# The last two experts' outputs combined on chip, the next layer's first weights and the sums loaded under the last products, a second buffer for the last activations

## The chip, the cores and the metric

One core of a Trainium2 chip runs the whole program in one launch. The metric is the device time of one execution in microseconds (us). The kernel before takes 1949.7 us, the median of three runs (1946.35 to 1953.62).

## The reference, cut to what matters

Two layers of a backbone, each a token mixer (three groups of heads) and an expert-choice channel mixer, run for 512 latent and 128 context tokens of width 1024. The change lies in the channel mixer and in the layer norm behind it:

```python
def _expert_choice(h, w_router, w_gate_up, w_down):
    aff = jax.nn.softmax((h @ w_router).astype(F32), axis=-1)
    gate, idx = lax.top_k(jnp.swapaxes(aff, 1, 2), cap)      # 16 experts; 64 latent, 16 context tokens each
    def per_request(hb, ib, gb):
        xe = hb[ib]
        a, b = jnp.split(jnp.einsum('ecd,edf->ecf', xe, w_gate_up), 2, axis=-1)
        ye = jnp.einsum('ecf,efd->ecd', jax.nn.silu(a) * b, w_down) * gb[..., None].astype(hb.dtype)
        return jnp.zeros_like(hb).at[ib.reshape(-1)].add(ye.reshape(-1, hb.shape[-1]))
...
x = _layernorm(alpha * x + g2 * ff, ln2_g[l], ln2_b[l])      # then the next layer's projection of x
```

## The kernel before, in words

All weights are float32 and come from HBM in tiles of 128x2048 (1 MB), into a pool of 25 slots (`Slots`); `Halves` hands out halves of a slot. `Ahead` holds the list of tiles to come; `fill(n, keep)` issues loads on SP's queue as long as fewer than n are held and more than `keep` slots are free. A slot is free again when its last matmul is done.

**The experts** (`moe`). For each of 16 experts e (e0 to e15): POOL gathers its 80 token rows by an indirect DMA (`gather`), VectorE turns them (`turned_x`, in 32x32 blocks, `squares`), `gate_up` multiplies them with eight tiles of gate and up weights (`wgu`) into PSUM, and ScalarE and VectorE make the activations `act`. One expert later, `turned_act` turns them into `aTs`, the only buffer for turned activations, and `down` multiplies with four tiles `wdn` into two PSUM banks `pl` (latent) and `pc` (context). `lat` (L1681) are the latent matmuls, `cxt` (L1685) the context ones. `down` ends on VectorE: gate and modulation for the latent half (L1739), for the context half (L1743, L1746), all into `y`. POOL adds `y` to the running sums `acc` in HBM by an indirect DMA with addition (L1754). `down(e-1)` is issued behind `gate_up(e)`.

**The last expert** before the change is not scattered. Its `y` is split into a high and a low part (`split`, L344 on ScalarE and L345 on VectorE) and added on chip: `combine(t)` makes each of the five token tiles t in PSUM as identity times `acc` (L1834, L1832) plus a one-hot matrix times `yh` (L1835) and `yl` (L1836). The one-hot rows come from comparing an `iota` table with the chosen indices (`places`, `one_hot`). The five tiles of `acc` are read back from HBM by SP's queue (L1814), behind the scatter of e14.

**The layer norm and the next layer's start** (`ln2`). Per tile: `ln_stats` (two bn_stats L608, bn_aggr L610, a reciprocal root on POOL L392, `nmr` L614), the normalisation on ScalarE (L1882), then behind layer 0 the turn by TensorE (L626), modulation (L631, L633) and a split (`hT_tile`: `hhi`, `hlo`, `hcx`; L344, L345), the store of x with its gains on POOL (L1902, L1905), and the first projection `tile_A` (L348 to L350) with the first weight tile of layer 1 (`first_w`: `win` split into `wh` and `wl` in four pieces). Behind layer 1 gains and offsets (L1884, L1885 on POOL and VectorE) and the stores to the outputs follow. `OR1` and `OR2` order these steps over the tiles.

What sets the order on an engine is the scheduler of the language, from the data and from `issue_after(x)`, which holds an instruction back until x has been issued. Each engine then works strictly in that order, and SP's queue too.

## Time and profile before

| what | value |
|---|---|
| median of three runs | 1949.7 us |
| the profiled execution's own time | 1953.35 us |
| its span, from first to last instruction | 1951.6 us |
| TensorE busy | 1807.9 us (93%) |
| VectorE, ScalarE, POOL busy | 1151.8, 417.7, 224.5 us |
| moved by DMA | 555 MB, 284 GB/s over the span |
| granted TensorE clock, mean | 0.957 of full |

The profiled execution is 3.65 us above the median, and 1.75 us of it lie around the span. A busy share is a mean over stages with different limits: in the experts' stage TensorE and the DMA engines are both full, and at the two ends of layers neither is.

### The profile page before, as it was taken

What the parts mean: (1) busy time and instruction counts of PE and PEld (TensorE: products, weight loads), DVE (VectorE), ACT (ScalarE), POOL (GpSimd) and SP (SyncE); (2) the same over time, 40 slices, a digit from 0 to 9 for tenths busy, and PEclk for the clock granted to TensorE, in tenths of its full rate; (3) what the DMA queues carried; (4) which work ended last, traced back from release to release, by engine and by line L of the source; (5) the groups of instructions that cost most, each with busy time, mean ns of one, the idle gap of its engine ahead of it and who ended that gap; (6) DMA issues with size and microseconds to landing.
All of it is one profiled execution on the core that took longest, in us unless ns stands there. A gap on an engine that the chain in (4) does not pass through costs nothing. (4 is left out here: it accounts for less than half of the span.)

```text
span 1951.6 us, 34372 instructions
## 1 busy us (share of the span) xinstructions
PE 1807.9 (93%) x14135; PEld 903.2 (46%) x14135; DVE 1151.8 (59%) x2966; ACT 417.7 (21%) x886; POOL 224.5 (12%) x176
## 2 busy tenths in 40 slices
PE   6999999868999999989879999989699999998995
PEld 3766767752333333323357667878223333332322
DVE  3654547568556585636386554675884657655356
ACT  2354533111000000000054654322100000000001
POOL 3200002101000110000062000130100101000003
PEclk9999999878999999999989999999699999999997
DMA  9343554488999999999545342247799999999973
GB/s 367 114 147 132 190 166 167 137 304 302 400 392 406 391 397 386 408 416 409 210 157 188 130 145 99 86 159 251 272 398 400 404 392 394 400 392 408 409 315 136
DMA packets 95980, 555.00 MB, mean 284 GB/s; under 512 B 13850, under 2 KB 18864, under 8 KB 36432
## 3 DMA queue, kind: packets, MB, share of 16 engines
q1 hardware_dynamic: 89104, 528.27, 68.9%
q0 software_dynamic: 6720, 24.54, 5.0%
q8 instruction: 111, 1.82, 0.4%
q14 instruction: 45, 0.37, 0.1%
HBM read 526.07 MB, written 26.70 MB: 283 GB/s over the span
## 5 line engine op out<-in xcount | busy, mean ns | idle before, releaser
L1681 PE MATMUL pA<-w,xT 128*32 128x512 f32 x4096 | 494.9, 605 | 24.3 <-DVE xT L1628 11.7
L1681 PEld LDWEIGHTS pA<-w,xT 128*32 128x32 f32 x4096 | 134.3, 112 | 340.6 <-issue 301.0
L1685 PE MATMUL pA<-w,xT 128*32 128x512 f32 x2048 | 270.0, 603 | 3.0 <-DVE xT L1652 3.0
L1681 PE MATMUL pB<-w,aT 128*32 128x512 f32 x2048 | 246.6, 598 | 5.7 <-issue 5.6
L1611 DVE STREAM_TRANSPOSE aT<-z 32x128 f32<-32x128 f32 x432 | 130.2, 301 | 53.2 <-PE pB L1681 27.6
L1681 PEld LDWEIGHTS pB<-w,aT 128*32 128x32 f32 x2048 | 69.9, 111 | 161.5 <-issue 146.6
L1685 PEld LDWEIGHTS pA<-w,xT 128*32 128x32 f32 x2048 | 68.1, 112 | 158.9 <-issue 153.3
L1685 PE MATMUL pB<-w,aT 128*32 128x512 f32 x1024 | 133.3, 593 | 0.0
L1611 DVE STREAM_TRANSPOSE aT<-turn 32x128 f32<-32x128 f32 x336 | 101.4, 302 | 25.3 <-PE pB L1681 19.4
L1715 DVE TENSOR_TENSOR z<-z,pA 128x512 f32<-128x512 f32 x18 | 12.4, 688 | 174.7 <-PE pA L1681 139.9
L348 PE MATMUL pA<-hhi,wh 128*128 128x512 f32 x224 | 92.1, 411 | 0.0
L1713 ACT ACTIVATE z<-pA 128x512 f32<-128x512 f32 x18 | 10.8, 598 | 376.6 <-PE pA L1681 376.6
L350 PE MATMUL pA<-hhi,wl 128*128 128x512 f32 x224 | 88.3, 396 | 0.5 <-DVE wl L345 0.5
L349 PE MATMUL pA<-hlo,wh 128*128 128x512 f32 x224 | 88.3, 394 | 0.0
L1685 PEld LDWEIGHTS pB<-w,aT 128*32 128x32 f32 x1024 | 35.6, 111 | 76.8 <-issue 75.0
L345 DVE TENSOR_TENSOR wl<-w,wh 128x1024 fp32r<-128x1024 f32 (+2 forms) x46 | 57.6, 1286 | 21.9 <-ACT wh L344 14.3
L348 PE MATMUL pA<-wh,cs 128*128 128x512 f32 x160 | 68.1, 428 | 1.9 <-ACT cs L344 1.9
L1713 ACT ACTIVATE turn<-pA 128x512 f32<-128x512 f32 x14 | 8.4, 597 | 274.3 <-PE pA L1681 274.3
L344 ACT ACTIVATE wh<-w 128x1024 fp32r<-128x1024 f32 (+2 forms) x50 | 53.8, 1121 | 51.9 <-DMA w<-win 29.3
L350 PE MATMUL pA<-wh,cs 128*128 128x512 f32 x160 | 64.2, 405 | 0.0
L349 PE MATMUL pA<-wl,cs 128*128 128x512 f32 x160 | 64.1, 401 | 0.0
L1754 POOL DMA_INDIRECT acc<-z,idx x16 | 23.5, 1466 | 343.6 <-DVE z L1746 326.8
(517 smaller groups left out, 2948.5 us busy)
## 6 DMA issues: line engine op xcount, KB each, us to landing
w<-wgu SPq DMA_DIRECT2D x256, 1024.0 KB, 19.9
w<-wdn SPq DMA_DIRECT2D x124, 1024.0 KB, 21.4
wada<-wada SPq DMA_DIRECT2D x48, 1024.0 KB, 5.0
w<-win SPq DMA_DIRECT2D x20, 1024.0 KB, 7.1
w<-wout SPq DMA_DIRECT2D x8, 1024.0 KB, 4.8
znd<-z SPq DMA_DIRECT2D x8, 512.0 KB
w<-wdn POOLq DMA_DIRECT2D x4, 1024.0 KB, 5.6
acc<-z SPq DMA_DIRECT2D x8, 512.0 KB, 3.3
```

What stands on the lines that cost most here:

```text
L344: hi_op[:] = [S.activation(hi[s], src[s], AF.Copy)]
L345: lo_op[:] = [E.tensor_tensor(lo[s], src[s], f32(hi[s]), op=ALU.subtract)]
L348: T.matmul(out, lh, rh, start=first, stop=False)
L349: T.matmul(out, lh, rl, start=False, stop=False)
L350: T.matmul(out, ll, rh, start=False, stop=last)
L1611: V.transpose(out, rows.rearrange("p (k q f) -> p k q f", q=4, f=32)[:, :, q, :])
L1681: T.matmul(p[32 * g:32 * g + 32], x[:, 64 * ko + 32 * i:64 * ko + 32 * i + 32], w[:, 512 * n:512 * n + 512], start=(ko == 0), stop=(ko == 7))
L1685: T.matmul(p[32 * g:32 * g + 32], x[:, 512 + 32 * ko:544 + 32 * ko], w, start=first, stop=last)
L1713: S.activation(act[:, 0:512], pl[0], AF.Silu)
L1715: V.tensor_mul(act[:, 0:512], act[:, 0:512], pl[1])
L1754: G.indirect_dma_start(out=acc[l], out_offset=IndirectOffsetOnAxis(ap=idx[:, e:e + 1], axis=0), in_=y[0:CAP, 0:1024], in_offset=None, comp ...
```

## The change

- Experts e14 and e15 are both added on chip. Their latent rows stand stacked in one 128-row pair `yh`, `yl`, their context rows in a 64-row pair `ch`, `cl`; the one-hot matrix has 128 rows for latent tokens and 64 for context tokens (`at` holds the indices, four small copies a layer). The scatter of e14 is gone.
- The five tiles of `acc` are read behind the scatter of e13, ahead of e14's products; identity times `acc` of tiles 0 and 1 (`begin`) stands on TensorE ahead of the one-hot products.
- The next layer's first weight tile is loaded right behind the last `wdn`, ahead of `acc`, and split under e15's products; two more follow `acc`.
- e15's turned activations have a buffer of their own (`last_aT`), and its products PSUM banks of tag A.

The cut diff:

```diff
         def turned_x(src):
-        def turned_act(act):
+        def turned_act(act, aTs=aTs):
...
         def down(e, aT):
-            last = e == NE - 1
-            y = hf.get(F32, "y")
-            yy = (hf.get(F32R, "yh"), hf.get(F32R, "yl")) if last else None
-            pl, pc = psB(), psB()
+            last = e - (NE - 2)
+            pl, pc = (psA(), psA()) if last == 1 else (psB(), psB())
...
+            if last >= 0:
+                on_chip(last, e, pl, pc, y)
+                return
...
+        def on_chip(i, e, pl, pc, y):
+            if i == 0:
+                for x in "LC":
+                    yk[x] = hf.get(F32R, "yh"), hf.get(F32R, "yl")
+            o, q = slice(64 * i, 64 * i + 64), slice(32 * i, 32 * i + 32)
+            (Lh, Ll), (Ch, Cl) = yk["L"], yk["C"]
+            for n in range(2):
+                r, c = slice(64 * n, 64 * n + 64), slice(512 * n, 512 * n + 512)
+                st_ = lambda: V.scalar_tensor_tensor(y[o, c], pl[r], gateL[r, e:e + 1], g2[r, 0:512],
+                                                     op0=ALU.mult, op1=ALU.mult)
+                with tc.issue_after((lo_op[0] if i and l + 1 < DEPTH else sq_last[0]).ins):
+                    st_()
+                S.activation(Lh[o, c], y[o, c], AF.Copy)
+            for n in range(2):
+                c = slice(512 * n, 512 * n + 512)
+                lo = V.tensor_tensor(Ll[o, c], y[o, c], f32(Lh[o, c]), op=ALU.subtract)
...
+                    V.scalar_tensor_tensor(yc[q, 512 * n:512 * n + 512], tC[r, 512:1024], gateC[r, e:e + 1],
+                                           g2[r, 512:1024], op0=ALU.mult, op1=ALU.mult)
+                split(Ch[q], Cl[q], yc[q])
...
-            V.tensor_scalar(hot[0][0:CAP, 0:NTOK], io[0:CAP, 0:NTOK], gsel[0:CAP, 1, NE - 1:NE], None,
-                            op0=ALU.is_equal)
+            at = fx.tile([128, 2], F32, name="at", tag="at")
+            for i in range(2):
+                e = NE - 2 + i
+                V.tensor_copy(at[64 * i:64 * i + 64, 0:1], gsel[0:64, 1, e:e + 1])
+                V.tensor_copy(at[32 * i:32 * i + 32, 1:2], gsel[64:96, 1, e:e + 1])
+            V.tensor_scalar(hot[0][:, 0:NLAT], io[:, 0:NLAT], at[:, 0:1], None, op0=ALU.is_equal)
+            V.tensor_scalar(hot[0][0:64, NLAT:NTOK], io[0:64, NLAT:NTOK], at[0:64, 1:2], None, op0=ALU.is_equal)
...
             act, aT, xT = gate_up(e, xT, prev, xgs[e + 1] if e + 1 < NE else None)
+            if e == NE - 1:
+                left = len(ahead.todo)
+                if l + 1 < DEPTH:
+                    ahead_layer(l + 1)
+                rest = ahead.todo[left + 1:]
+                del ahead.todo[left + 1:]
+                ahead.fill(99, 3)
+                hf.free(*xgb)
+                accs.extend([hf.get(F32, "acc") for _ in range(NT)])
+                for t in range(NT):
+                    sums = nc.sync.dma_start(accs[t], acc[l][128 * t:128 * t + 128])
+                last_aT = turned_act(act, hf.get(F32, "aT"))
             if prev is not None:
                 down(e - 1, aT)
...
-        ahead.fill(KF, 4)
-        yh, yl = down(NE - 1, turned_act(prev))
-        for t in range(NT):
-            sums = (G if SQ == "G" else nc.sync).dma_start(accs[t], acc[l][128 * t:128 * t + 128])
+        ahead.add(rest)
+        with tc.issue_after(sums.ins):
+            ahead.fill(KF, 4)
+            if l + 1 < DEPTH:
+                ahead.have.insert(0, ahead.have.pop(4))
+                first_ws[l + 1] = first_w(l + 1)
+            down(NE - 1, last_aT)
```

How it moves instructions, at the three places on which the terms rest (rows that only repeat one above them are left out). SP's queue at the end of layer 0, before (`w<-wdn` is the last expert's last tile, `tab`, `cak`, `ln` small tables of what follows, `win` the next layer's weights):

```order
L289 DMA w_7252<-wdn 128x2048
L1814 DMA z_3126<-acc_98 128x1024
L1814 DMA catB_1836<-acc_98 128x1024
L1814 DMA aT_3763<-acc_98 128x1024
L1814 DMA acc_7309<-acc_98 128x1024 x2
L289 DMA tab_7413<-tab 128x2048
L289 DMA work_7310<-cak 128x128
L289 DMA ln_339_7425<-ln2g 128x1024
L289 DMA ln_339_7425<-ln2b 128x1024
L289 DMA w_7843<-win 128x2048
```

And now:

```order
L289 DMA w_7256<-wdn 128x2048
L289 DMA w_7258<-win 128x2048
L1848 DMA catB_1836<-acc_98 128x1024
L1848 DMA turn_3873<-acc_98 128x1024
L1848 DMA z_3126<-acc_98 128x1024
L1848 DMA z_2971<-acc_98 128x1024 x2
L289 DMA w_7391<-win 128x2048
L289 DMA w_7405<-win 128x2048
L289 DMA tab_7439<-tab 128x2048
L289 DMA work_7353<-cak 128x128
```

The first `win` has moved ahead of the sums, and two more stand ahead of the small tables.

VectorE at the end of layer 0, before: the turn of e15's activations (`aT`) lies around the end of e14 (`catB` is its y), then e15's y (`z`), its split and the first statistics:

```order
L1739 SCALAR_TENSOR_TENSOR catB_1836<-pB,gateL,catB_1836 64x512 x2
L1611 STREAM_TRANSPOSE aT_3763<-z_3126 32x4x32 x3
L1719 TENSOR_TENSOR z_3126<-z_3126,turn_3873 64x512
L1611 STREAM_TRANSPOSE aT_3763<-z_3126 32x4x32 x9
L1743 TENSOR_TENSOR turn_3873<-pB,turn_3873 64x512
L1746 SCALAR_TENSOR_TENSOR catB_1836<-turn_3873,gateC,catB_1836 16x512 x2
L1739 SCALAR_TENSOR_TENSOR z_3126<-pB,gateL,catB_1836 64x512 x2
L1743 TENSOR_TENSOR yC_7389<-pB,yC_7389 64x512
L1746 SCALAR_TENSOR_TENSOR z_3126<-yC_7389,gateC,catB_1836 16x512 x2
L345 TENSOR_TENSOR yl_7336<-z_3126,onehot_6437 80x1024
L608 BN_STATS bs<-pA 128x6
L345 TENSOR_TENSOR kA_7414<-work_7310,kA_7414 128x128
```

And now (`turn` is e15's own buffer, `aT` and `xg` e14's y, `wl` the first weight tile's low part, `z` e15's y from the banks A):

```order
L1615 STREAM_TRANSPOSE turn_3873<-z_3126 32x128 x8
L1769 SCALAR_TENSOR_TENSOR aT_3763<-pB,gateL,catB_1836 64x512 x2
L1776 TENSOR_TENSOR yl_7339<-aT_3763,onehot_6437 64x512 x2
L1781 TENSOR_TENSOR xg_3764<-pB,xg_3764 64x512
L345 TENSOR_TENSOR wl_7356<-w_7258,wh_7355 128x512 x2
L1784 SCALAR_TENSOR_TENSOR xg_3764<-xg_3764,gateC,catB_1836 32x512 x2
L345 TENSOR_TENSOR yl_7340<-xg_3764,yl_7339 32x1024
L1769 SCALAR_TENSOR_TENSOR z_3126<-pA,gateL,catB_1836 64x512 x2
L1776 TENSOR_TENSOR yl_7339<-z_3126,onehot_6437 64x512 x2
L1781 TENSOR_TENSOR aT_3763<-pA,aT_3763 64x512
L1784 SCALAR_TENSOR_TENSOR z_3126<-aT_3763,gateC,catB_1836 32x512 x2
L610 BN_STATS bs<-pA 128x6 x2
```

All 24 blocks of e15's turn stand ahead of e14's y; the weight tile's low part stands between e14's y and e15's; the piece `kA`, which waits for the small table `cak`, has left this place for one behind the third tile's statistics.

POOL at the same place, now (before, the scatter of e14 stood at its head, and `hlo` behind three of the long products with gains):

```order
L1755 DMA acc_98<-z_2971,idx 640x1024
L392 TENSOR_TENSOR rs_7486<-rsv_7487,half 128x1
L1962 TENSOR_TENSOR catB_1836<-catB_1836,ln_340_7451 128x1024
L1962 TENSOR_TENSOR y_341_7635<-turn_3873,ln_340_7451 128x1024
L1965 TENSOR_TENSOR catB_1836<-catB_1836,ln_340_7451 128x1024
L345 TENSOR_TENSOR hlo_7448<-work_7353,hhi_7446 128x4x128
L1965 TENSOR_TENSOR y_341_7635<-y_341_7635,ln_340_7451 128x1024
L1962 TENSOR_TENSOR turn_3873<-z_3126,ln_340_7451 128x1024
L1965 TENSOR_TENSOR turn_3873<-turn_3873,ln_340_7451 128x1024
```

The long products with gains (L1962, L1965) now follow the first norm closely, and still stand ahead of the first tile's `hlo`.

## Rows read from the trace of the kernel before

**Rows 1.** The page: the DMA row of its second part.
```profile
DMA packets 95980, 555.00 MB, mean 284 GB/s; under 512 B 13850, under 2 KB 18864, under 8 KB 36432
```

**Rows 2.** Windows: from:to, length, busy per engine (PE, PEld, DVE, ACT, POOL), clock, DMA, GB/s.
```profile
950.00:955.00 5.00, 3.73 (x14) 1.16 (x18) 4.72 (x14) 0.00 (x0) 0.00 (x0) 0.66 0.00 0
```

**Rows 3.** Timeline, TensorE, end of layer 0: start, length, what [idle before <-releaser].
```profile
937.97 1.90 PE L1681 MATMUL pB<-w,aT 128*32 128x512 f32 x16
...
947.41 1.04 PE L1685 MATMUL pB<-w,aT 128*32 128x512 f32 x8
951.27 7.36 PE L1681 MATMUL pB<-w,aT 128*32 128x512 f32 x44 [2.82 <-issue]
...
968.86 2.07 PE L1834 MATMUL pA<-z,cst 128*128 128x512 f32 x2 [4.62 <-DMA z<-acc]
...
1016.22 0.42 PE L350 MATMUL pA<-wh,hcx 128*128 128x256 f32 x1 [1.67 <-DVE hcx L345]
```

**Rows 4.** Timeline, VectorE, end of layer 0.
```profile
954.47 3.82 DVE L1611 STREAM_TRANSPOSE aT<-z 32x128 f32<-32x128 f32 x12
...
963.42 1.53 DVE L1739 SCALAR_TENSOR_TENSOR z<-pB,gateL,catB 64x512 f32<-64x512 f32 x2 [3.60 <-PE pB L1681]
...
968.33 1.22 DVE L345 TENSOR_TENSOR yl<-z,onehot 80x1024 fp32r<-80x1024 f32 x1 [1.12 <-ACT onehot L344]
971.82 0.70 DVE L608 BATCH_NORM_STATS2 bs<-pA 128x6 f32<-128x512 f32 x1 [2.27 <-PE pA L1836]
977.68 0.29 DVE L345 TENSOR_TENSOR kA<-work,kA 128x128 fp32r<-128x128 f32 x1 [5.16 <-DMA ln<-ln2g]
...
979.70 0.21 DVE L614 TENSOR_SCALAR nmr<-mv,rs 128x1 f32<-128x1 f32 x1 [0.69 <-POOL rs L392]
...
986.36 1.71 DVE L345 TENSOR_TENSOR wl<-w,wh 128x512 fp32r<-128x512 f32 x2 [1.93 <-ACT wh L344]
...
988.60 3.92 DVE L345 TENSOR_TENSOR wl<-w,wh 128x512 fp32r<-128x512 f32 x2
...
1013.99 2.17 DVE L345 TENSOR_TENSOR hcx<-work,hcx 128x512 fp32r<-128x512 f32 x1
```

**Rows 5.** SP's waits (us in total, times, longest), and timeline rows of POOL, SP, ScalarE.
```profile
SPq L1814 <- DMA acc<-catB,idx: 40.0, 1, 40.0
...
925.52 1.40 POOL L1754 DMA_INDIRECT acc<-z,idx  x1 [30.72 <-DVE z L1746]
...
907.38 17.71 SPq L289 DMA_DIRECT2D w<-wdn  x8
...
970.73 1.61 SPq L289 DMA_DIRECT2D w<-win  x2
...
985.70 2.19 ACT L344 ACTIVATE wh<-w 128x512 fp32r<-128x512 f32 x4 [1.74 <-DMA w<-win]
```

**Rows 6.** Timeline, VectorE and POOL at the same time, the first tiles of layer 1.
```profile
1003.91 1.28 DVE L345 TENSOR_TENSOR hlo<-work,hhi 128x512 fp32r<-128x512 f32 x2
...
1005.75 2.41 DVE L345 TENSOR_TENSOR hlo<-work,hhi 128x512 fp32r<-128x512 f32 x1
...
1005.20 2.42 POOL L1902 TENSOR_TENSOR z<-aT,ln 128x1024 f32<-128x1024 f32 x1 [6.71 <-DMA xres<-z]
```

**Rows 7.** Timeline, the end of layer 1: TensorE, VectorE, ScalarE, POOL.
```profile
1900.18 9.08 PE L1681 MATMUL pB<-w,aT 128*32 128x512 f32 x60 [2.82 <-issue]
...
1912.34 1.53 DVE L1739 SCALAR_TENSOR_TENSOR z<-pB,gateL,catB 64x512 f32<-64x512 f32 x2 [3.61 <-PE pB L1681]
...
1925.60 1.45 ACT L1882 ACTIVATE z<-pA,nmr,rs 128x512 f32<-128x512 f32 x2 [8.38 <-DVE nmr L614]
...
1926.45 2.50 POOL L1884 TENSOR_TENSOR z<-z,ln 128x512 f32<-128x512 f32 x2 [1.28 <-ACT z L1882]
...
1941.68 3.05 POOL L1885 TENSOR_TENSOR acc<-acc,ln 128x512 f32<-128x512 f32 x2
...
1945.21 1.28 DVE L1885 TENSOR_TENSOR acc<-acc,ln 128x512 f32<-128x512 f32 x2
```

More of the change, by code (lines that the diff above doesn't have):

```diff
@@ L1607, in moe @@
         bufs = [xTs[:, 0:768], xTs[:, 1024:1792]]
+        sq_last = []
         def squares(out, rows, q):
-            V.transpose(out, rows.rearrange("p (k q f) -> p k q f", q=4, f=32)[:, :, q, :])
+            sq_last[:] = [V.transpose(out, rows.rearrange("p (k q f) -> p k q f", q=4, f=32)[:, :, q, :])]
         def turned_x(src):
@@ L1748, in down @@
             hf.free(tC)
-            if last:
-                split(yy[0][0:CAP], yy[1][0:CAP], y[0:CAP])
-                sl.free(xTs)
-                hf.free(y, aTs)
-                return yy
             G.indirect_dma_start(out=acc[l], out_offset=IndirectOffsetOnAxis(ap=idx[:, e:e + 1], axis=0),
@@ L1756, in down @@
             hf.free(y)
+        def on_chip(i, e, pl, pc, y):
[14 more added lines that the diff above has]
+                lo = V.tensor_tensor(Ll[o, c], y[o, c], f32(Lh[o, c]), op=ALU.subtract)
+            hf.free(y)
+            tC, yc = hf.get(F32, "yC"), hf.get(F32, "yc")
+            S.activation(tC[0:64, 0:512], pc[64:128], AF.Copy)
+            with tc.issue_after(lo.ins):
+                V.tensor_tensor(tC[0:64, 512:1024], pc[0:64], tC[0:64, 0:512], op=ALU.add)
+                for n in range(2):
+                    r = slice(32 * n, 32 * n + 32)
+                    V.scalar_tensor_tensor(yc[q, 512 * n:512 * n + 512], tC[r, 512:1024], gateC[r, e:e + 1],
+                                           g2[r, 512:1024], op0=ALU.mult, op1=ALU.mult)
+                split(Ch[q], Cl[q], yc[q])
+            hf.free(tC, yc)
+        yk = {}
         def keep(e):
@@ L1764, in places @@
             hot.append(hf.get(F32, "iota"))
-            ld(hot[0][0:CAP, 0:NTOK],
-               bass.AP(tensor=a["iota"].tensor, offset=a["iota"].offset, ap=[[0, CAP], [1, NTOK]]))
+            ld(hot[0][:, 0:NTOK], bass.AP(tensor=a["iota"].tensor, offset=a["iota"].offset, ap=[[0, 128], [1, NTOK]]))
         def one_hot():
@@ L1798, in moe @@
             init(7, x_last[1])
+            if e == NE - 1:
[5 more added lines that the diff above has]
+                ahead.fill(99, 3)
+                assert not ahead.todo
+                hf.free(*xgb)
[3 more added lines that the diff above has]
+                last_aT = turned_act(act, hf.get(F32, "aT"))
             if prev is not None:
@@ L1819, in moe, with begin @@
                 sl.free_ = sl.free_[-LF:] + sl.free_[:-LF]
-            if WB != 2:
-                ahead_layer(l + 1)
         c_last = []
+        sums_of = {}
+        def begin(t):
+            ps_ = sums_of[t] = []
+            for n in range(2):
+                p = {"A": psA, "B": psB, "C": psC}[(PB if l + 1 < DEPTH else P2)[t]]()
+                if c_last:
+                    with tc.issue_after(c_last[-1]):
+                        T.matmul(p, ident, accs[t][:, 512 * n:512 * n + 512], start=True, stop=False)
+                else:
+                    T.matmul(p, ident, accs[t][:, 512 * n:512 * n + 512], start=True, stop=False)
+                ps_.append(p)
```

43 lines of the change are left out of this document (20 added, 23 removed).

## The prediction, made before the change was run

> **What bounds the kernel now.** I read the windows first, then the timelines of TensorE and VectorE where a layer ends, then SP's waits. In the experts' stage TensorE and the DMA engines are full together, so nothing that only shortens VectorE or POOL work there shows. The change works at two places where neither is full: the end of layer 0 with the start of layer 1, and the end of the kernel.
>
> At the end of layer 0 the reader is to see a chain with holes. e14's products end at 948.45 (947.41 plus 1.04); e15's start at 951.27, after a hole of 2.82, because its activations are turned on VectorE around e14's output, up to 958.29 (954.47 plus 3.82) [rows 3, 4]. From 950 to 955 the granted clock is 0.66, so part of these products runs at 1.2 instead of 2.4 GHz, and the DMA engines move nothing [rows 2]. SP has waited 40.0 us for the scatter of e14, with the sums, the small tables and the next weights queued behind that wait, in this order [rows 5]. e15's output starts at 963.42 on VectorE; the one-hot sums wait 4.62 for `acc` and start at 968.86; the first norm has its figures (`nmr`) at 979.70, VectorE having stood 5.16 at `kA`, a piece that needs a small table [rows 3, 4]. The first weights are issued at 970.73 and reach ScalarE at 985.70 [rows 5]; their low part then takes VectorE 1.71 and 3.92 [rows 4]. From there VectorE sets the pace: TensorE waits 1.67 for `hcx`, whose split ends at 1016.16, and is dense behind it [rows 3, 4]. I use that split as the marker: what it moves, the rest of layer 1 moves.
>
> **The sum, part by part.**
>
> *A: e15's products.* A second buffer lets all blocks of e15's turn stand ahead of e14's output. e14's four tiles of weights took 937.97 to 948.45, 10.5 us [rows 3]. With no hole and no slow clock, e15's take the same and end at 948.3 plus 10.5, 958.8; the latent half, done 0.9 earlier, lets the output start at 957.9 instead of 963.42. **5.5 us.** The weights are no bound: the last eight tiles are issued from 907.38 on, within 17.71 [rows 5], and the windows show the DMA engines idle before 950. What e14's output does on VectorE from 947.7 on (two gate steps 1.53, split, add, two context steps 1.53, split 1.22, with the next weights' low part at the unstretched price of 1.71 for two, 3.4 in all) adds up to some 10 us [rows 4], so it ends at 957.6 to 958, just in time.
>
> *B: from e15's output to the first norm's figures.* Before: 979.70 minus 963.42, 16.3. Now, with sums and identity products done ahead: gate 1.53, two low parts of some 0.65 each (half of the 1.22 row, for about half the elements), an add of the same, context steps 1.53, its split 1.22, six bn_stats at 0.70 (three tiles now stand ahead of the first `nmr`), small steps at 0.21 each, five of them: 1.5+1.3+0.7+1.5+1.2+4.2+1.1 = 11.5, and some 0.6 of waits between engines, 12.1 [rows 4]. **4.2 us**, so `nmr` at 970.0. The added wait: SP's reads of `acc` now wait for e13's scatter, issued at 925.52 and queued in POOL's 1.40 [rows 5]. Behind it stand two weight tiles and the small tables; they are needed only after 970, so 20 us of delay there would cost nothing. The first weight tile and the sums, 3.5 MB, are issued behind 925.09 at the pace of the last eight tiles (17.71 for 8 MB), by 933, and with the 15 us that a weight tile took from issue to use (970.73 to 985.70) they are there by 948 [rows 5].
>
> *C: from there to the marker.* Before 979.70 to 1016.16, 36.5. Moved out: the low part 1.71 and 3.92 and its wait of 1.93, four bn_stats 2.8; moved in `kA`, 0.3 [rows 4]. That leaves 26.4. Against it stands POOL. Two `hlo` splits took 1.28 together while POOL was still; one that met a POOL product of 2.42 took 2.41 and ended with it [rows 6]. The low part's 3.92 is the same. Of the nine such splits of VectorE before, about four were stretched. Now the ten long POOL products follow the first norm without a break, so up to five more splits can be stretched by 2.41 minus 0.64, 1.8 each, 8.9 in all: 26.4 to 35.3. With nothing to tell them apart I take half, 30.8. **5.7 us** (1.2 to 10.1).
>
> The Trainium skill ("SBUF — State Buffer", Who interferes with whom) has this as a rule: an instruction of VectorE with two SBUF inputs and one of GpSimd (POOL) that reads SBUF exclude each other, and the later one blocks until the other ends. It speaks against this change; the row of 2.41 agrees with it, and by the rule alone all nine would wait and C would be 35.3.
>
> *D: the end of the kernel.* e15's products start at 1900.18 after the same hole, its output at 1912.34, and the first norm at 1925.60 [rows 7]. A again gives 5.4 (1906.9), B's sum 12.0 to the first norm (1918.9), 6.7 earlier. From there the ten half-tile products each of POOL and VectorE set the end: before 1925.60 to 1946.49 (1945.21 plus 1.28), 20.9. Now both statistics of tiles 0 and 1 are ready together, so POOL need not stand between its products: ten at 1.25 to 1.53 (2.50 and 3.05 for two) [rows 7], three small roots and a start of 1 give 15 to 19; I take 17.2. **10.4 us** (6.5 to 12.5). The drain behind the last instruction stays.
>
> *E: what is added elsewhere.* Eight copies of one column, for which the nearest row is `nmr`, 0.21 [rows 4]: 0 if hidden, 1.7 if all lie on the way to the gathers. Two `iota` loads grow by 48 rows, 0.25 MB together: at the mean of 284 GB/s [rows 1] 0.9 at most, where the DMA engines are full; two scatters less give some back. One-hot rows and gate steps have the same row length on more partitions, nothing. **1.0 us lost** (0 to 2.6).
>
> Sum: 5.5 + 4.2 + 5.7 + 10.4 - 1.0 = 24.8. The profiled execution of 1953.35 would take 1928.6. It stands 3.65 above the median of the runs; against that, 1949.7 minus 24.8, **1925 us**. About 0.5%, 10 us, can be told from no change.
>
> **The rivals.**
>
> *POOL takes the gain back at the layer's start.* All splits meet POOL, C gives 1.2, and at the end POOL's and VectorE's products meet as well, D 6.5: 5.5 + 4.2 + 1.2 + 6.5 - 1.0 = 16.4, 1933. For it: the order of POOL, and the 2.41 row. Against: some splits fall between POOL's products, as four or five did before. 0.20. The rule of the Trainium skill quoted above ("SBUF — State Buffer") would make it this outcome.
>
> *POOL costs no more than before.* C 10.1, D 12.5: 31.7 with E at 0.6, 1918. For it: POOL's `hlo` and roots break its row of products, and layer 1's later splits of weights then meet a POOL that is done. 0.16.
>
> *The change does not do what it says: the sums come late.* If `acc` is read only when e15's products are done, the first sums are some 3.6 later (the 4.62 of before less their start) at both ends: 24.8 - 7 = 18, 1932. For it: eight weight tiles ahead of them on the queue. Against: the idle DMA engines from before 950. 0.06.
>
> *Slower: the weight tile that now stands inside the chain comes late.* Its low part stands on VectorE ahead of e14's context half and of all of e15's output, its high part on ScalarE ahead of the same. VectorE reaches it at about 951.4; each us that the tile is later moves the whole start of layer 1. Before, such a tile took 15 us from issue to use (970.73 to 985.70) [rows 5]. At 976 the whole gain would be gone, from 986 on the kernel would be slower by over 0.5%; at 990, 1963. Against: the load is the next on the queue behind tiles issued by 925.09, and would have to wait 46 us after them. 0.02.
>
> **How the numbers follow.** The forecast, 1920 to 1930, has 0.56. The range leaves out the slower rival and the rest of 0.02 with worse mixes: from 1917 (all upper bounds, 33) to 1934 (all lower ones, 15), and 3 us more on either side, since the median of before is itself known to some 3.6: 1913 to 1938. Faster by over 0.5% (below 1940) holds for all cases but the slower one and the worst mixes: 0.93; within 0.5% 0.05; slower 0.02.
>
> **What would show it.** Right: no hole on TensorE between e14's and e15's products and a clock of 1.0 there; sums and first weights landed before 955; the first `nmr` near 970 (less what the run is shifted as a whole); the marker 15 us earlier; the kernel's last instruction some 10 us nearer to e15's products than before, taken from e14's. Wrong: ScalarE or VectorE waiting at the weight split for a DMA; `hlo` rows of over 2 us each; a wait for `cak` behind the third tile; or a gain far from 15 and 10 at the two ends.

## The result, and the profile after

The changed kernel takes **1923.4 us** (median of four runs, 1922.07 to 1927.15) against 1949.8 for the kernel before: a ratio of **0.9864**, 95% interval 0.9844 to 0.9885, 26.4 us faster. The profiled execution of after took 1923.11 with a span of 1921.3; before it was 1953.35 and 1951.6, so the two spans differ by 30.3, and those 30.3 are what can be followed instruction by instruction.

TensorE at the end of layer 0, in the changed kernel (columns as in [rows 3]; in after `lat` is L1685, `cxt` L1689, the identity products L1883):

```profile
935.21 1.90 PE L1685 MATMUL pB<-w,aT 128*32 128x512 f32 x16
...
944.65 1.04 PE L1689 MATMUL pB<-w,aT 128*32 128x512 f32 x8
945.51 4.90 PE L1685 MATMUL pA<-w,turn 128*32 128x512 f32 x43
...
955.95 1.98 PE L1883 MATMUL pA<-catB,cst 128*128 128x512 f32 x4
...
998.95 0.38 PE L350 MATMUL pA<-wh,hcx 128*128 128x256 f32 x1 [0.99 <-DVE hcx L345]
```

The hole of 2.82 of [rows 3] is gone: e15's products stand right behind e14's, and the identity products of the sums behind those, with no wait for `acc` (4.62 before). The window 950 to 955 (columns of [rows 2]) shows the other half of it, clock 1.00 in place of 0.66 and busy DMA engines in place of idle ones:

```profile
950.00:955.00 5.00, 5.00 (x52) 1.71 (x47) 4.22 (x6) 1.70 (x3) 0.00 (x0) 1.00 0.98 379
```

VectorE in the same stretch, changed kernel, to set beside [rows 4]:

```profile
955.21 1.53 DVE L1769 SCALAR_TENSOR_TENSOR z<-pA,gateL,catB 64x512 f32<-64x512 f32 x2 [0.94 <-PE pA L1685]
...
966.32 0.35 DVE L616 TENSOR_SCALAR nmr<-mv,rs 128x1 f32<-128x1 f32 x2
...
973.39 2.89 DVE L345 TENSOR_TENSOR hlo<-work,hhi 128x512 fp32r<-128x512 f32 x1 [0.99 <-ACT hhi L344]
...
979.67 0.74 DVE L345 TENSOR_TENSOR hlo<-work,hhi 128x512 fp32r<-128x512 f32 x1
...
990.89 2.42 DVE L345 TENSOR_TENSOR hlo<-work,hhi 128x512 fp32r<-128x512 f32 x1 [0.54 <-ACT hhi L344]
...
996.97 1.93 DVE L345 TENSOR_TENSOR hcx<-work,hcx 128x512 fp32r<-128x512 f32 x1
```

e15's output starts 20.0 us after e14's products (955.21 minus 935.21; before 963.42 minus 937.97, 25.45); `nmr` follows 11.1 later (16.3 before); the marker, the end of the first `hcx` split, at 998.90 is 32.6 after `nmr` (36.5 before). The splits of 0.7 us that take 1.26 to 2.89 are those that start while one of POOL's products runs:

```profile
968.68 2.35 POOL L1962 TENSOR_TENSOR catB<-catB,ln 128x1024 f32<-128x1024 f32 x1
...
973.38 2.35 POOL L1965 TENSOR_TENSOR catB<-catB,ln 128x1024 f32<-128x1024 f32 x1
...
990.41 2.36 POOL L1965 TENSOR_TENSOR z<-z,ln 128x1024 f32<-128x1024 f32 x1
...
995.63 2.71 POOL L1965 TENSOR_TENSOR z<-z,ln 128x1024 f32<-128x1024 f32 x1
```

Set side by side, the ends show that such a split is not slowed but waits: it ends some 0.55 us after the product that was running when it started (976.28 against 975.73, 993.31 against 992.77, 998.90 against 998.34). In all nine stretched splits of before and after the distance is 0.54 to 0.56.

The queues, beside [rows 5]: the first weight tile is issued at 925.64, the sums from 932.24, and ScalarE, after waiting 1.06 for it, splits that tile at 948.46, 22 us before it was even issued in the kernel before (970.73):

```profile
925.64 0.33 SPq L289 DMA_DIRECT2D w<-win  x1
932.24 0.33 SPq L1848 DMA_DIRECT2D catB<-acc  x1
...
948.46 2.19 ACT L344 ACTIVATE wh<-w 128x512 fp32r<-128x512 f32 x4 [1.06 <-DMA w<-win]
```

The end of the kernel (ScalarE's first norm, VectorE's and POOL's last products), beside [rows 7]:

```profile
1885.41 1.53 DVE L1769 SCALAR_TENSOR_TENSOR z<-pA,gateL,catB 64x512 f32<-64x512 f32 x2 [2.43 <-PE pA L1685]
...
1896.71 1.45 ACT L1942 ACTIVATE catB<-pA,nmr,rs 128x512 f32<-128x512 f32 x2 [4.57 <-DVE nmr L616]
...
1904.41 5.73 DVE L1944 TENSOR_TENSOR z<-z,ln 128x512 f32<-128x512 f32 x4 [0.34 <-ACT z L1942]
...
1913.45 2.35 DVE L1945 TENSOR_TENSOR z<-z,ln 128x512 f32<-128x512 f32 x2
...
1908.25 6.39 POOL L1945 TENSOR_TENSOR z<-z,ln 128x512 f32<-128x512 f32 x4
```

First norm to VectorE's last end: 1915.80 minus 1896.71, 19.1, against 20.9.

### The profile page after: what moved, and what is told of

Read it like the earlier page. It is cut to its first block, busy times and chain, and to the rows that moved or that the text cites. A ratio compares the mean times of both kernels' runs of the same rounds, so it can differ in the third digit from the quotient of the medians.

```text
span 1921.3 us, 34400 instructions
## 1 busy us (share of the span) xinstructions
PE 1788.8 (93%) x14135; PEld 912.4 (47%) x14135; DVE 1157.5 (60%) x2986; ACT 423.5 (22%) x896; POOL 221.8 (12%) x174
## 4 chain that ended last, share of the span: by engine, by line
PE 72%; DMA 17%; DVE 6%; issue 3%; ACT 2%; POOL 1%; SPq 0%; DVEq 0%; POOLq 0%; ACTq 0%
PE pA L1685 18%; DMA w<-wgu 10%; PE pA L1689 8%; PE pA L348 7%; PE pB L1685 7%; PE pA L349 6%; PE pA L350 6%; DMA w<-wdn 5%; PE pB L1689 4%; PE pB L356 2%; PE pC L813 2%; PE pA L517 2%; PE pA L917 1%; PE pB L1395 1%; PE pB L491 1%
## 5 line engine op out<-in xcount | busy, mean ns | idle before, releaser
L1685 PE MATMUL pA<-w,xT 128*32 128x512 f32 x4096 | 496.4, 603 | 24.8 <-DMA w<-wgu 12.6
L1685 PEld LDWEIGHTS pA<-w,xT 128*32 128x32 f32 x4096 | 142.9, 111 | 331.4 <-issue 288.4
L1689 PE MATMUL pA<-w,xT 128*32 128x512 f32 x2048 | 270.7, 600 | 3.0 <-DVE xT L1656 3.0
L1685 PE MATMUL pB<-w,aT 128*32 128x512 f32 x1920 | 227.1, 592 | 1.3 <-DMA w<-wdn 1.3
L1615 DVE STREAM_TRANSPOSE aT<-z 32x128 f32<-32x128 f32 x384 | 115.7, 301 | 51.2 <-PE pB L1685 27.3
L1689 PEld LDWEIGHTS pA<-w,xT 128*32 128x32 f32 x2048 | 72.4, 111 | 154.0 <-issue 148.2
L1685 PEld LDWEIGHTS pB<-w,aT 128*32 128x32 f32 x1920 | 67.1, 110 | 141.0 <-issue 126.2
L1689 PE MATMUL pB<-w,aT 128*32 128x512 f32 x960 | 124.1, 592 | 0.0
L1689 PEld LDWEIGHTS pB<-w,aT 128*32 128x32 f32 x960 | 33.7, 110 | 69.4 <-issue 66.5
L1719 DVE TENSOR_TENSOR turn<-turn,pA 128x512 f32<-128x512 f32 x14 | 9.6, 688 | 88.4 <-PE pA L1685 88.3
```

The source lines that it names most:

```text
L1615: sq_last[:] = [V.transpose(out, rows.rearrange("p (k q f) -> p k q f", q=4, f=32)[:, :, q, :])]
L1685: T.matmul(p[32 * g:32 * g + 32], x[:, 64 * ko + 32 * i:64 * ko + 32 * i + 32], w[:, 512 * n:512 * n + 512], start=(ko == 0), stop=(ko == 7))
L1689: T.matmul(p[32 * g:32 * g + 32], x[:, 512 + 32 * ko:544 + 32 * ko], w, start=first, stop=last)
L1719: V.tensor_mul(act[:, 0:512], act[:, 0:512], pl[1])
```

## The experiments

Each was timed against the kernel before on its own chip, whose time there gives the ratio. The stages come from each kernel's profiled execution: **B'** from ScalarE's first step on e15's activations (1.5 us ahead of e14's products) to the first `nmr`; **C** from there to the marker; **M** from the marker to ScalarE's layer-norm step of layer 1 (`lngb`), most of the mixer; **R** from there to layer 1's first `nmr`; **End** from that to the end of the span. What is left of a span, the stretch ahead of B', took 933.0 to 936.5 us; no edit is aimed at it.

| kernel | median us | ratio (95%) | B' | C | M | R | End |
|---|---|---|---|---|---|---|---|
| before | 1949.8 | 1 | 43.2 | 36.5 | 321.3 | 587.8 | 26.4 |
| after | 1923.4 | 0.9864 (0.9844 to 0.9885) | 32.6 | 32.6 | 316.1 | 581.4 | 24.9 |
| e1 one buffer | 1931.0 | 0.9894 (0.9878 to 0.9911) | 35.6 | 36.3 | 316.6 | 583.9 | 24.9 |
| e2 late weights | 1939.5 | 0.9940 (0.9924 to 0.9956) | 35.0 | 33.2 | 328.2 | 580.3 | 24.9 |
| e3 e14 scattered | 1946.8 | 0.9987 (0.9974 to 1.0) | 34.0 | 35.7 | 330.6 | 582.1 | 24.7 |
| e10 e3, tables mended | 1927.6 | 0.9893 (0.9867 to 0.9919) | 33.9 | 36.2 | 316.0 | 579.6 | 25.0 |
| e4 plain store | 1939.3 | 0.9943 (0.9927 to 0.9960) | 32.6 | 26.5 | 329.9 | 586.2 | 24.9 |
| e5 before + buffer, order, banks | 1928.1 | 0.9878 (0.9858 to 0.9899) | 32.7 | 36.0 | 316.3 | 579.4 | 25.8 |
| e9 before + early scatter | 1958.8 | 1.0033 (1.0018 to 1.0048) | 44.7 | 38.9 | 318.1 | 597.6 | 26.6 |
| e6 tile 0 first | 1921.2 | 0.9840 (0.9818 to 0.9862) | 29.6 | 32.5 | 320.8 | 577.1 | 26.7 |
| e7 split from PSUM | 1919.6 | 0.9831 (0.9811 to 0.9850) | 32.6 | 29.2 | 315.6 | 580.2 | 24.9 |
| e8 end in PSUM | 1916.6 | 0.9822 (0.9800 to 0.9844) | 32.6 | 32.6 | 317.6 | 580.0 | 19.2 |
| e11 e6 + e7 + e8 | 1921.7 | 0.9846 (0.9823 to 0.9868) | 29.6 | 33.3 | 317.3 | 585.9 | 22.3 |
| e12 e7 + e8 | 1912.1 | 0.9806 (0.9785 to 0.9827) | 32.6 | 29.6 | 316.2 | 579.1 | 19.2 |

### One part of the change undone (e1 to e4)

**e1**, the changed kernel with a single buffer; e15's turn is issued behind e14's products and ahead of its output.

```diff
+            if then:
+                then()
             y = hf.get(F32, "y")
...
-                last_aT = turned_act(act, hf.get(F32, "aT"))
+                then = lambda: turned_act(act)
```

> The changed kernel with e15's activations turned into the buffer that e14's products read; their blocks still stand ahead of e14's output on VectorE. Theory (term A): the 24 blocks, 6.71 us, can then start only behind e14's last product, so TensorE has a hole of 2 to 4 us between e14's and e15's products at the end of each layer, the granted clock falls there, and e15's output comes some 5 us later at each of the two ends: 1933 us (1930 to 1936) against 1923.4 of the change. Rival: e15's output is gated by the queue of e14's output on VectorE (which ends 0.94 us before e15's products do), so a hole of the same length costs nothing more than the order: 1926 or less.

1931.0, 7.6 above the changed kernel (the intervals just overlap). The time lies in the expected range, but not for the expected reason: TensorE has **no hole** here. TensorE and VectorE of e1:

```profile
934.42 1.90 PE L1685 MATMUL pB<-w,aT 128*32 128x512 f32 x16
...
944.73 5.75 PE L1685 MATMUL pA<-w,aT 128*32 128x512 f32 x51
...
944.10 5.10 DVE L1615 STREAM_TRANSPOSE aT<-z 32x128 f32<-32x128 f32 x16 [1.89 <-PE pB L1685]
949.23 1.53 DVE L1771 SCALAR_TENSOR_TENSOR turn<-pB,gateL,catB 64x512 f32<-64x512 f32 x2
```

e14's products start at 934.42, e15's at 944.73, without a wait. So one buffer is enough to close the hole, if e15's turn stands ahead of e14's output on VectorE and e15's products have other banks. The banks belong to it: e14's output begins to read its own, `pB`, only at 949.23, 4.5 us after e15's products start, and there are just two of that tag. No run has the new order with the old banks, or the order and the banks with nothing else. What the single buffer costs lies on VectorE: the turn can only follow the products that free its blocks and ends at 949.2 instead of 944.1, so e14's output starts 14.8 us after e14's products instead of 9.7, e15's output 2.4 later, `nmr` 3.0 later, and C is 3.7 longer.

**e2**, the first weights loaded and split behind e15's products, as before.

```diff
-                rest = ahead.todo[left + 1:]
+                rest = ahead.todo[left:]
...
-                first_ws[l + 1] = first_w(l + 1)
...
-            w = first_ws[l + 1]
+            w = first_w(l + 1)
```

> The changed kernel with the next layer's first weights loaded behind the sums and split in the place of before (after the one-hot sums have begun). Theory: the four low parts, 2.6 us when nothing stands against them, come back between e15's output and the marker, on the engine that sets the pace there; only the end of layer 0 is touched: 1926 to 1927 us, marker 3 us later. Rival 1: they meet POOL's products as before (5.6 us): 1929. Rival 2: VectorE has 3 us of waits between the first norm and the first split of h, which take them up: 1923 to 1924, and the early load was worth nothing. Rival 3: the small tables stand behind more weight tiles on the queue and kA waits for its table again, as in the 5.16 us of before: 1928 or more.

1939.5, 16 us above the changed kernel. Only 3 of it are where the split stands: the low parts take VectorE 2.50 between the statistics, `nmr` is 2.4 later and the marker 0.6 more. The rest is behind the marker: M is 12.1 longer, which none of the expectations had. Three rows, VectorE and TensorE of e2:

```profile
964.12 2.50 DVE L345 TENSOR_TENSOR wl<-w,wh 128x512 fp32r<-128x512 f32 x4
...
1009.88 0.50 PE L350 MATMUL pA<-hhi,wl 128*128 128x512 f32 x1 [2.58 <-DVE wl L328]
...
1020.46 1.58 PE L356 MATMUL pB<-kA,qA 64*128 64x256 f32 x12 [5.18 <-ACT qA L344]
```

TensorE waits 2.58 for the low part of a later weight tile and then 5.18 for `qA`; another such split on VectorE waited 2.40 for the store of a token tile. e2 moved the whole list of tiles by one, and how much of the 12 is slots and how much the queue's order was not separated.

**e3**, e14 scattered again, the sums read behind its scatter.

```diff
-            if last >= 0:
+            if last == 1:
                 on_chip(last, e, pl, pc, y)
...
+            if e == NE - 1:
+                for t in range(NT):
+                    sums = nc.sync.dma_start(accs[t], acc[l][128 * t:128 * t + 128])
```

> The changed kernel with e14 scattered as all experts before it and only e15 combined on chip; the second buffer, the order of e15's turn and the early first weights stay. The reads of acc then wait for e14's scatter again. Theory: e14's output ends near 950, its scatter and a read of acc take some 9 us as before (960.10 to 968.86), so the first identity products start near 958.5 instead of 955.95, still ahead of e15's low parts (958.7): 0 to 2 us per layer end, 1924 to 1927. Rival: the sums wait for acc as before, 4.6 us, and the small tables behind them make kA wait 5 us more: 1933 or more, and combining e14 on chip would be the larger part of the gain.

1946.8, nearly all of the gain gone; but the profile says it is not the scatter. SP, POOL and TensorE of e3:

```profile
958.50 2.54 SPq L289 DMA_DIRECT2D w<-win  x4
...
980.44 2.40 POOL L1965 TENSOR_TENSOR catB<-catB,ln 128x1024 f32<-128x1024 f32 x1 [0.36 <-DMA ln<-ln2g]
...
1012.27 4.37 DVE L345 TENSOR_TENSOR kA<-turn,kA 128x384 fp32r<-128x384 f32 x2 [0.59 <-ACT kA L344]
...
1026.08 2.01 ACT L344 ACTIVATE wh<-w 128x1024 fp32r<-128x1024 f32 x2 [13.64 <-DMA xres<-z]
...
1019.02 0.80 PE L350 MATMUL pA<-hhi,wl 128*128 128x512 f32 x1 [9.97 <-DVE wl L328]
```

With the sums late, four weight tiles of 1 MB now stood ahead of the small tables on SP's queue. POOL's row of products waited for `ln2g`, started at 980.44 instead of 968.68 and ran into the mixer, until 1016.5. There two splits of `kA` took VectorE 4.37 (0.76 in the changed kernel), TensorE waited 9.97 for the weight split `wl` behind them, and ScalarE waited 13.64 for the store of a token tile before it could split a later weight tile; M is 14.5 longer. **e10** takes that side effect away: the same edit, with the tables put ahead of the weights.

```diff
-        ahead.add(rest)
         with tc.issue_after(sums.ins):
-            ahead.fill(KF, 4)
...
             down(NE - 1, last_aT)
+        ahead.add(rest)
```

> The kernel with e14 scattered (e3) once more, with the order of loads mended: the further weight tiles of the next layer are put on the queue behind the small tables, not ahead of them. Theory: what cost e3 its 23 us was the tables behind four weight tiles (POOL's first gain waited for them until 980.4), not the sums' wait for the scatter; with the tables in front it comes to 1922 to 1927, and combining e14 on chip is worth 0 to 4 us by itself. Rival: the wait for the scatter is the cost, 1935 or more.

1927.6: M is back at 316.0, and the ratio is 0.9893. Combining e14 on chip, beside a second buffer and early weights, is worth 0.3% (some 5.6 us; the intervals overlap, and the order of the loads differs too), not the 23 that e3 alone suggested.

**e4**, the plain x stored; its gain products move out of POOL's row at the layer's start into the next mixer. Everything is still computed.

```diff
-RZ = 0
+RZ = 1
```

> The changed kernel with the plain norm stored at the end of layer 0 and its gains put on by POOL where the mixer of layer 1 loads it: the ten long POOL products leave the start of layer 1. Theory (POOL stretches VectorE's splits): no split of h between the first norm and the marker takes over 1.5 us, and the stretch from the first nmr to the marker falls from 32.5 to some 26.5 us; the whole gains those 6 us less what the moved products cost later: 1918 to 1923. Rival: that stretch is set by the steps between ScalarE, TensorE and VectorE, and stays within 1 us of 32.5; the time is that of the change or above.

C falls to 26.5, within 0.1 of the 26.4 that the prediction had for a POOL that is out of the way, and the splits take 0.68 to 0.69. The time is nevertheless 1939.3, outside what either theory said: M is 13.8 longer than in the changed kernel, and TensorE waits for e15's input in layer 1, so that R is 4.8 longer. VectorE and TensorE of e4:

```profile
994.20 0.68 DVE L345 TENSOR_TENSOR hcx<-work,hcx 128x512 fp32r<-128x512 f32 x1
...
1856.76 3.42 PE L1685 MATMUL pA<-w,xT 128*32 128x512 f32 x16 [7.36 <-DVE xT L1632]
```

### The second buffer alone (e5), the order without it (e9)

**e5** is the kernel before with a second buffer, e15's turn ahead of e14's output, and other PSUM banks for e15. e14 is still scattered, the sums are still read behind its scatter, and the first weights are still split in their old place, after e15's output.

```diff
+            if e == NE - 1:
+                last_aT = turned_act(act, hf.get(F32, "aT"))
             if prev is not None:
...
-        yh, yl = down(NE - 1, turned_act(prev))
+        yh, yl = down(NE - 1, last_aT)
```

> The kernel before, with nothing of the change but the second buffer: e15's activations get their own, all their blocks stand ahead of e14's output on VectorE, and e15's products go to psA (in psB they would wait for e14's output to be read). e14 is still scattered, the sums and the first weights are loaded as before. Theory (term A alone): e15's products stand right behind e14's and e15's output comes 5.5 us earlier at each of the two ends: 1940 us (1937 to 1943) against 1951 before. Rival 1: e14's output and its scatter come earlier too (the scatter went out at 960.10, behind the turn; now near 951), so all that waits for the sums moves by up to 9 us at the end of layer 0: 1935 or less. Rival 2: the reads of acc and the small tables behind them set the start of layer 1 whatever TensorE does: 1944 or more.

Ratio 0.9878, some 23.8 of the 26.4 us: its first rival came true, not the 1940 of term A. What the other two parts of the change add to it is 0.14%, 2.7 us, with overlapping intervals; in the stages it is 3.4 in C. The reason can be read off POOL in the kernel before:

```profile
960.10 1.40 POOL L1754 DMA_INDIRECT acc<-catB,idx  x1 [33.19 <-DVE catB L1746]
...
982.14 2.35 POOL L1902 TENSOR_TENSOR catB<-z,ln 128x1024 f32<-128x1024 f32 x1
```

and off POOL, SP, ScalarE, TensorE and VectorE in e5:

```profile
948.48 1.40 POOL L1757 DMA_INDIRECT acc<-turn,idx  x1 [24.77 <-DVE turn L1749]
...
968.78 2.37 POOL L1907 TENSOR_TENSOR kT<-aT,ln 128x1024 f32<-128x1024 f32 x1
...
935.03 0.33 SPq L289 DMA_DIRECT2D w<-win  x1
...
953.41 0.33 SPq L1819 DMA_DIRECT2D aT<-acc  x1
...
971.86 2.18 ACT L344 ACTIVATE wh<-w 128x512 fp32r<-128x512 f32 x4
...
957.37 1.10 PE L1839 MATMUL pA<-aT,cst 128*128 128x512 f32 x2 [1.82 <-DMA aT<-acc]
...
966.00 0.21 DVE L614 TENSOR_SCALAR nmr<-mv,rs 128x1 f32<-128x1 f32 x1 [0.69 <-POOL rs L392]
```

With e14's output no longer among and behind the turns, its scatter goes out at 948.48 instead of 960.10. The 40 us wait of SP's queue [rows 5] ends 12 us earlier, and everything behind it moves: the sums and the small tables (the 5.16 at `kA` is gone). One load moved that was not meant to: the first weight tile went out at 935.03, ahead of that wait, instead of 970.73 behind it, and ScalarE split it at 971.86 without waiting (985.70, after 1.74, before). e5 is therefore not free of early weights, and what this load gives was not priced apart; C is only 0.5 shorter than before. POOL starts its row at 968.78 instead of 982.14, and `nmr` stands where the changed kernel has it (966.00, 966.32).

**e9**: is it the scatter, then, and not the buffer? The kernel before with one buffer, e15's turn issued only behind the whole of e14's output.

```diff
-        yh, yl = down(NE - 1, turned_act(prev))
+        with tc.issue_after(out_last[0].ins):
+            last_aT = turned_act(prev)
+        yh, yl = down(NE - 1, last_aT)
```

> The kernel before with one order changed: e14's output stands in one piece ahead of the blocks of e15's turn on VectorE; one buffer as before. e14's scatter can then go out near 951.5 instead of 960.10, while e15's products start no earlier. It tells whether the gain of the second buffer came from TensorE's hole or from the scatter at the head of the queues. Theory (both, and the larger part from e15's products and output): the wait for acc (4.62) and that for the small table (5.16) go, e15's output stays at 963.4, the first nmr comes 4 to 6 us earlier: 1942 to 1946 us against 1951. Rival: the scatter alone makes the gain, the hole on TensorE is covered by it: 1928 to 1933.

Slower, 1.0033, which neither its theory nor its rival had. Rows of VectorE, POOL and TensorE in e9, the last from layer 1:

```profile
949.15 7.66 DVE L1611 STREAM_TRANSPOSE aT<-z 32x128 f32<-32x128 f32 x24
...
968.21 0.29 DVE L345 TENSOR_TENSOR kA<-work,kA 128x128 fp32r<-128x128 f32 x1 [3.39 <-ACT kA L344]
...
949.40 1.40 POOL L1756 DMA_INDIRECT acc<-catB,idx  x1 [25.50 <-DVE catB L1748]
...
950.50 6.43 PE L1681 MATMUL pB<-w,aT 128*32 128x512 f32 x37 [5.07 <-issue]
...
1871.26 5.37 PE L1681 MATMUL pA<-w,xT 128*32 128x512 f32 x27 [7.36 <-DVE xT L1628]
```

The scatter is as early as in e5 (949.40), but the whole turn now stands between the products: TensorE's hole is 5.07, e15's output is later, and B' is 1.5 longer than before. That e9 is slower than before has another cause, though. R is 9.8 longer: in layer 1 VectorE finishes e15's input late, and TensorE waits 7.36 for it, as in e4 and e11, so that from ScalarE's first step for e14 to that for e15 pass 40.6 us instead of 32.3. Without these 8.3 the span of 1959.3 would be 1951.0, that of before 1951.6. So the early scatter gains nothing as long as e15's products are late for it; a loss of its own it does not show.

### What bounds the rest (e6, e7, e8, e11, e12)

**e6**, the changed kernel with e15's context half put behind the first `nmr`.

```diff
+            if i:
+                yk["later"] = lambda: (context(nm_last[0]), hf.free(g2))
+            else:
+                context(lo.ins)
```

> The changed kernel with another order on VectorE at the two ends of layers: the statistics of tile 0 as soon as its sums are there, then nmr of tile 0, and only then the context half of e15's output (0.68, 1.50 and 1.22 us) and the statistics of tile 1. Nothing is left out. Theory: the first nmr comes 3.5 us earlier at both ends (11.1 us from e15's output become 7.6); VectorE's waits of some 3 us behind it (1.16, 0.28, 0.51, 0.99) take up the moved work, so the marker comes 2 to 3 us earlier and the end of the kernel 1 to 3: 1917 to 1920 us. Rival: VectorE's work and POOL's products set the marker and the end, not the first nmr: 1922 to 1924.

`nmr` comes 3.0 earlier and the marker too, but nothing of it can be told in the time (0.9840 against 0.9864): M is 4.7 longer, and POOL's row of gain products ends where it did (998.33 against 998.34). At the other end R is 4.3 shorter, 2.9 of it by the earlier `nmr`, and End, with VectorE and POOL both full behind the first norm, takes 1.8 back.

**e7**, token tiles that VectorE scales are scaled in place in PSUM, so that the low-part split has one operand in PSUM.

```diff
-            w = work()
+            w = work() if E is G else p
```

> The changed kernel with the turned tiles of h scaled in place in PSUM, so that VectorE's splits of h at the start of layer 1 read one operand from PSUM and one from SBUF, not two from SBUF; POOL's ten long products stay where they are. Theory (two SBUF operands against a POOL product): no split takes over 1.2 us though POOL is busy, and the stretch from the first nmr to the marker falls from 32.5 to 26.5 to 28 us, as it did when the POOL products were taken away (26.5): 1916 to 1919 us. Rival 1: the splits are stretched by POOL whatever they read: 32 to 33, 1923. Rival 2: the two PSUM tiles are held longer, and TensorE's transposes wait for them: 29 to 34 with short splits, 1920 to 1925.

VectorE of e7:

```profile
975.08 0.69 DVE L345 TENSOR_TENSOR hlo<-pC,hhi 128x512 fp32r<-128x512 f32 x1 [1.06 <-ACT hhi L344]
...
987.68 0.42 DVE L635 TENSOR_SCALAR pC<-pC,GBT 128x128 f32<-128x128 f32 x1 [1.33 <-PE pC L628]
...
996.41 0.69 DVE L345 TENSOR_TENSOR hcx<-pC,hcx 128x512 fp32r<-128x512 f32 x1 [0.55 <-ACT hcx L344]
```

Every split takes 0.68 to 0.69 beside POOL's products, and these are shorter too, 2.36 to 2.42 instead of 2.34 to 2.83. C falls only to 29.2, not to 26.5 (the second rival), since VectorE now waits for turned tiles of TensorE (1.33, 0.60, 0.58) and for ScalarE.

**e8** does the same at the end: the norm stays in PSUM for the tiles that VectorE multiplies, and the additions of one more tile go from POOL to VectorE.

```diff
-EA = 4
+EA = 3
...
+                out = z[n] if h is None and t >= EM else x[:, s]
+                S.activation(out, z[n], AF.Identity, scale=rs, bias=nm)
```

> The changed kernel with another end of layer 1: the norm of tiles 1 to 4 is written in place in PSUM, VectorE multiplies from there (one operand from SBUF instead of two), and the second gain of tile 3 goes from POOL to VectorE. Theory: VectorE's ten products at the end, 13.9 us now (1.76, 1.65, 5.73 for four, 2.36 and 2.35 for two), take some 0.7 us each, and from the first norm to the last instruction pass 13 to 16 us instead of 19.1: 1918 to 1920 us. Rival: POOL's own row (ten products of 1.25 and five roots, 17 us now) sets the end, and with two products less it gives back 2.5 at most: 1921 to 1923.

VectorE of e8, its last products:

```profile
1903.86 1.37 DVE L1946 TENSOR_TENSOR pC<-pC,ln 128x512 f32<-128x512 f32 x2
...
1908.64 1.28 DVE L1947 TENSOR_TENSOR z<-pA,ln 128x512 f32<-128x512 f32 x2
```

A half tile takes 0.64 to 0.69 instead of 1.2 to 1.4; first norm to VectorE's last end is 13.4 (19.1), End 19.2. POOL also has two products less, and what each half of the edit gave was not separated.

**e11** puts e6, e7 and e8 together, **e12** only e7 and e8:

```diff
-EA = 4
+EA = 3
...
-            w = work()
+            w = work() if E is G else p
```

> The changed kernel with the three orders of e6, e7 and e8 together: statistics of tile 0 first, splits of h from PSUM, the end of layer 1 from PSUM. Theory: they act one behind the other (3 us before the first nmr, some 3 between it and the marker, 5 to 6 at the end, and the earlier first norm of layer 1, which POOL and VectorE took back in e6, counts now that VectorE's products are short): 1907 to 1912 us. Rival: the gains overlap, since each fills the same waits of VectorE: 1914 or more.

> The changed kernel with the edits of e7 and e8 alone (splits of h from PSUM at the start of layer 1, the end of layer 1 from PSUM), without the order of e6. Theory: e11 lost its gain to an order of VectorE that its third edit brought about (the input of e15 in layer 1 turned 7.4 us too late, a hole on TensorE) and to the overlap of e6 and e7 in the same stretch; without that edit the gains of e7 (some 3 us) and e8 (5 to 6) stand at two places and add up: 1912 to 1916 us. Rival: they do not add, 1917 or more, as the single runs of e7 and e8.

e11 adds nothing to e8 (1921.7). e6 and e7 fill the same waits (B' and C together: 65.2 in the changed kernel, 62.1 in e6, 61.8 in e7, 62.9 in e11), and in layer 1 VectorE's order changed: e15's input came behind turns that wait for TensorE. TensorE of e11:

```profile
1851.59 5.35 PE L1685 MATMUL pA<-w,xT 128*32 128x512 f32 x27 [7.36 <-DVE xT L1632]
```

**e12 takes 1912.1** (1909.87 to 1916.49), 0.9806 of before, clear of the changed kernel's interval: the fastest kernel here. The two edits add up: by the spans 11.4 together (1921.3 minus 1909.9), 3.5 and 5.9 alone. At their own places, C and End, they give 3.0 and 5.7; 2.3 more lie in R, where no edit is.

## Why the prediction was right, and where it was not

The forecast of 1925 (1913 to 1938) was 1.6 us off. That it is so close is partly luck: in the profiled pair, which the sum was made for, the gain is 30.3 and not 24.8. The account there, from mark to mark:

| step | predicted | found |
|---|---|---|
| ahead of e14's products | 0 | 2.8 |
| A, to e15's output | 5.5 | 5.45 |
| B, to the first `nmr` | 4.2 | 5.2 |
| C, to the marker | 5.7 (1.2 to 10.1) | 3.9 |
| marker to the end of e14's products in layer 1 | 0 | 4.2 |
| D, from there to the end | 10.4 | 8.8 |
| E, added work | -1.0 | not seen |

**A** was right to 0.1 us: no hole, a clock of 1.00, output at 20.0. But its cause was put too narrowly. The step read "a second buffer lets all blocks of e15's turn stand ahead of e14's output"; e1 shows that the order and the other banks close the hole with one buffer. e15's output starts 22.4 after e14's products there, so of the 5.45 the second buffer is worth 2.4.

**B**: right, 1.0 too small. The early sums did what the step said. ScalarE waited 1.06 for the weight tile, until 948.46; the step had it there "by 948", and such a wait was named as a sign of being wrong, but it moved nothing behind it: VectorE still waits 0.94 for TensorE at e15's output. The rival of a late weight tile and the rival of late sums are both answered by these rows and by `acc`, for which TensorE has no wait.

**C**: the mechanism was right and its size off. The term took half of five additional stretched splits, 30.8; measured 32.6. Of nine splits (seven `hlo`, two `hcx`) six took 1.26 to 2.89, four of the `hlo` over 2 us, which was named as a sign of being wrong, and `kA` 1.29 instead of 0.3. Before it was three of nine (2.41, 2.67, 2.17), not "about four", so six more could have been stretched and not five. The one of 2.41 did not end with POOL's product, as the prediction has it, but 0.54 after it (1008.16 against 1007.62). The stretching itself came out near the 4.4 that the term took for it: 3.7 in the splits up to the marker, 1.0 in `kA`. The other 1.5 are waits and steps that the term did not price. e4 shows the lower bound (26.5 with POOL's products away), e7 that the operand decides: with one operand in PSUM no split is stretched. The Trainium skill ("SBUF — State Buffer", Who interferes with whom) also says that a VectorE instruction with at most one SBUF input does not contend with GpSimd, outside the 2-port performance modes. e7's 0.69 beside POOL's products agrees. The prediction's upper bound of 35.3 had all nine splits wait; here two found POOL between two products (979.67, 984.09), and a third came behind its last one and behind the marker (999.22).

**D**: the part of A came (5.5), that of B gave 2.0 where 1.3 was expected, but the last stage gave 1.8 of 3.7 and the drain took 0.4 more. The term added up POOL's products at 1.25 to 1.53 and took 17.2 out of 15 to 19; in the trace VectorE's end last, and the two engines stretch each other (6.39 for four of POOL's, 5.73 for four of VectorE's, of which two took 1.28 in [rows 7]). The lower bound of 6.5, given for the case that they meet, was too low all the same: it leaves the last stage no gain. e8, where VectorE reads from PSUM and POOL has two products less, needs 13.4.

**Not in the sum**: 2.8 ahead of the change's place and 4.2 behind the marker. The 4.2 go with POOL's row, which ends at 998.3, ahead of the marker, where before it ended 13 behind it, at 1028.9. M is 315.6 to 317.6 in the kernels where that row ends ahead of the marker (the changed one, e1, e5, e7, e8, e10, e11, e12) and 318.1 to 321.3 where it ends 2 to 13 behind it (e9, e6, before); e2, e3 and e4 have losses of their own there. That fits, but no run tested it. The 2.8 need be no effect of the change: most of it is one expert, e13, which took 37.5 instead of 39.6 in this pair and varies as much from trace to trace. Against the medians, the profiled run of before stood 3.65 high; that is why 30.3 in the spans is 26.4 in the medians, and why, with 7.0 outside the sum and its terms 1.5 short, the forecast is off by only 1.6.

**The step that failed** is the division of the gain among the parts. The prediction priced the second buffer as A alone, 5.5 at either end, and gave B, C and the other half of D to the sums and weights loaded early and to the combination on chip. e5 scatters e14, reads the sums behind that scatter, splits the first weights late, and keeps 23.8 of 26.4; of the early loads it has only the issue of the first weight tile. The prediction had the row for it ([rows 5], SP waiting 40.0 for the scatter of e14) and did not ask what that scatter waited for: e14's output, which stood among e15's turns. One late output held the scatter, the scatter held the queue, and the queue held sums, tables and weights. The change attacks this chain twice, by letting the output go early and by needing no scatter, and either does most of it: the buffer with its order and banks gives 0.9878 (e5), everything but the buffer 0.9894 (e1), both 0.9864. Prices of parts do not add where they cure the same wait. What stays open is the share of e15's order and banks, which e1, e5 and e10 all have and no run has alone.

## What to carry to other kernels

Follow a long wait of a queue back to what its releaser itself waited for before you price its cures one by one; two edits that free the same chain are worth little more than the better one. When a part is undone to price it, look behind its own place: e2's and e3's losses lay mostly in the next stage (M, 12.1 and 14.5), e3's from small tables behind large tiles, and e10 gave back 19 us by the order of loads. e4, e9 and e11 each lost some 8 us a whole layer later, at an input that VectorE finished late. Where VectorE and POOL share a stretch, leave one operand of VectorE's products in PSUM, as e7, e8 and e12 did.
